# Plain weight tiles of a hybrid decoder layer: rounded by a transfer, with the low part made by a negation and an accumulating transfer, in place of a float32 tile that two engines split

## The chip, the core and the metric

The kernel runs on one core of a Trainium2 chip, in one launch. The metric is device time in microseconds, as the median of three runs. Profiles come from one profiled execution; its span runs from the first to the last instruction, and the time of that execution is a little longer.

## What is computed

One decoder layer over 16 meta tokens and 512 tokens (T = 528 columns, features on the partitions), d_model 1024, all in float32:

```python
h = h + 0.5 * swiglu(rmsnorm(h, norm_ffn1), w_ffn1_in, w_ffn1_out)      # d_ff 2816
u = rmsnorm(h, norm_mix)
fq, fk, fv, ff, rq, rk, rv, rg, ga, gb = split(u @ w_in)
y_a = forgetting_attention(qknorm(fq), qknorm(fk), fv, cumsum(log_sigmoid(ff + b)))   # 16 heads of 64
y_b = silu(rg) * head_groupnorm(retention(rotary(rq), rotary(rk), rv))                # 4 heads
h = h + (sigmoid(ga) * (y_a @ w_o_fox) + sigmoid(gb) * (y_b @ w_o_ret)) @ w_out
h = h + 0.5 * swiglu(rmsnorm(h, norm_ffn2), w_ffn2_in, w_ffn2_out)
```

The meta tokens stand ahead of the sequence; the output is that of the 512 tokens.

## The kernel before

**Products.** Each float32 operand is held as two float32r tiles: the high part (`wh`, `xh`), which is the value rounded, and the low part (`wl`, `xl`), the rest. A product is three matmuls, high by high, high by low and low by high (`mm3`, line 269, and `mm3s`, line 285). A weight piece of 1024 columns holds eight k-steps of 128; over 528 columns, in two ranges of 272 and 256, it makes 48 matmuls, over 512 columns 24.

**Weights.** All weights are cut beforehand into a list of `loads` (up to 2048 columns, kind "w" for plain or "S" for those of a Strassen-like scheme in the two SwiGLU blocks) and a list of `pieces` in the order in which TensorE takes them (lines 125 to 162). Two plain pieces make up a load of 2048 columns. `load` (line 168) brings a load as float32 into a raw tile, with SP's queue, into one of two buffers of 8 KB per partition for plain loads (tag `w`) or of two for Strassen loads (tag `wS`). `ready` (line 195) prepares the pieces up to a number: for a plain piece `split` (line 104) rounds the raw piece into `wh` on ScalarE (line 105) and subtracts on VectorE into `wl` (line 106); Strassen pieces are split in halves of 512 columns, from the raw tile or from sums that VectorE makes (`wsums`, line 184). `wh` and `wl` have four buffers each. `weights` (line 219) is called once for each piece that TensorE takes, and readies pieces up to two ahead of it.

**Order.** TensorE's order is written out by hand (`SEQ` at line 36 for the SwiGLU blocks; generators woven by costs, `weave` at line 112, for attention and retention). The other engines' orders come from a planner that takes what is ready by order of tracing, and each engine and each issuing queue runs its list in order. At the very start ScalarE's and VectorE's orders too are as traced (line 478). In the token list a and b are plain pieces of the input weights, e and l stand for two Strassen pieces each (24 matmuls per piece), and p is a piece of the output weights (640 or 768 columns).

**Names.** `fpa`, `fpb`, `fq`, `fpo` are products of the first SwiGLU block, `spa`, `sq`, `spo` those of the second; `pff`, `pq`, `pk`, `pv`, `pg`, `prq` to `prg` are projections; `q0pm`, `k0pm` the means of the q and k norms; `pzt`, `pzd` transposes in the forget gate's chain (`forget`, line 533), `z`; `S`, `P`, `PT`, `PV` attention's scores, softmax, transposes and outputs, with `ph`, `pl` the split of P transposed; `oa`, `ob`, `ow` the products with w_o_fox, w_o_ret and w_out.

**GpSimd's queue** makes constants at the start, the bias tiles of attention (`bias`, line 760: a load `B` from `negc` and an addition `Bd`), the loads of stored gates (`gate`, line 1033: `gs` from `gsp`) and of the stored residual (line 1092: `hh` from `hsp`).

**The start.** The first load, w0, comes in four quarters of 512 columns that alternate with the tiles of h on SP's queue (lines 234 to 238); n0 takes pieces 0 and 1 side by side, n1 takes pieces 2 and 3.

Of the kernel before, what the change touches and what calls it, by code (L numbers as in the profile page):

```python
# [17 lines left out]
F32 = mybir.dt.float32  # L18
F32R = mybir.dt.float32r
AF = mybir.ActivationFunctionType  # L20
ALU = mybir.AluOpType
# [4 lines left out]
S = 512  # L26
# [38 lines left out]
def layer(tc, order, hT, wf1i, wf1o, wf2i, wf2o, wmix, wsq, vecs, cs, rmask, rvec, cmask, outT):  # L65
    nc = tc.nc
    PSUM = bass.MemoryType.PSUM
    PE = mybir.EngineType.PE
    with ExitStack() as es:
        cp = es.enter_context(tc.tile_pool(name="const", bufs=1))  # L70
        wp = es.enter_context(tc.tile_pool(name="w", bufs=1))
        ap = es.enter_context(tc.tile_pool(name="a", bufs=1))
        tp = es.enter_context(tc.tile_pool(name="t", bufs=1))
        sp = es.enter_context(tc.tile_pool(name="sm", bufs=1))
# [10 lines left out]
        def atile(name, dt=F32):  # L85
            return ap.tile([128, T], dt, name=name, tag="a", bufs=NA)
# [4 lines left out]
        def f32(x):  # L91
            return x.bitcast(F32)
# [11 lines left out]
        def split(xh, xl, src):  # L104
            nc.scalar.activation(xh, src, AF.Copy)  # L105
            nc.vector.tensor_tensor(xl, src, f32(xh), ALU.subtract)  # L106
# [18 lines left out]
        loads = []  # L125
        pieces = []
# [8 lines left out]
        def feed_ffn(seq, w_in, w_out):  # L135
            at_, nxt = {}, [0] * len(PJ)
            for tok in seq:
                c, j = tok[0], int(tok[1:])
                if c == "u":
                    continue  # L140
                if c == "p":
                    n = PJ[j] * 128
                    m = nxt[j]
                    nxt[j] += 1
                    if m % 2 == 0:
                        loads.append((w_out[j * 4 + m // 2], 2 * n, "w"))
                        at_[tok] = len(loads) - 1
                    pieces.append((at_[tok], m % 2 * n, n))
                    continue
                if c in "nae":  # L150
                    loads.append((w_in[j], 2048, "S" if c == "e" else "w"))
                    at_[j] = len(loads) - 1
                cuts = {"n": [0, 1024], "a": [0], "b": [1024],
                        "e": [("A0", "S1"), ("A2", "S0")], "l": [("A1", "S2"), ("A3",)]}[c]
                pieces.extend((at_[j], x, 1024) for x in cuts)
# [4 lines left out]
        for i in range(3 * KC // 2):  # L160
            feed(wsq[i], [1024, 1024])
        feed_ffn(SEQ, wf2i, wf2o)
        raw, sums, got = {}, {}, {}
        u = [], []
        st = {"sp": None}
        at = {"l": 0, "p": 0, "u": 0}

        def load(n):
            while at["l"] < min(n, len(loads)):
                i = at["l"]  # L170
                src, w, kind = loads[i]
                if kind == "S":
                    if st["sp"] is None:
                        return
                    raw[i] = st["sp"].tile([128, 2048], F32, name=f"w{i}", tag="wS", bufs=2)
                else:
                    raw[i] = wp.tile([128, 2048], F32, name=f"w{i}", tag="w", bufs=2)
                ld = nc.sync.dma_start(raw[i][:, :w], src[:, :w])
                if i == 5:
                    with tc.issue_after(ld.ins):  # L180
                        nc.sync.dma_start(RV, rvec)
                at["l"] += 1

        def wsums(i):

            a11, a12, a21, a22 = (raw[i][:, 512 * x:512 * x + 512] for x in range(4))
            sums[i] = st["sp"].tile([128, 1536], F32, name=f"ws{i}", tag="ws", bufs=1)
            s1, s2, s4 = (sums[i][:, 512 * x:512 * x + 512] for x in range(3))
            with tc.issue_after(st["sq"].ins):
                nc.vector.tensor_tensor(s1, a21, a22, ALU.add)  # L190
            nc.vector.tensor_tensor(s2, s1, a11, ALU.subtract)
            nc.vector.tensor_tensor(a21, a11, a21, ALU.subtract)
            nc.vector.tensor_tensor(s4, a12, s2, ALU.subtract)

        def ready(n):
            while at["p"] < min(n, len(pieces)):
                i = at["p"]
                li, c, w = pieces[i]
                load(li + 2 if i >= 2 else 1)
                if li not in raw:  # L200
                    return
                if loads[li][2] == "S" and li not in sums:
                    wsums(li)
                wh = wp.tile([128, 1024], F32R, name=f"wh{i}", tag="wh", bufs=4)
                wl = wp.tile([128, 1024], F32R, name=f"wl{i}", tag="wl", bufs=4)
                got[i] = wh, wl
                at["p"] += 1
                if i < 2:
                    for x in (0, 512):
                        split(wh[:, x:x + 512], wl[:, x:x + 512], raw[li][:, c + x:c + x + 512])  # L210
                        gained(2 * i + x // 512, gn1, u, 0, "n1")
                elif loads[li][2] == "S":
                    for x, src in enumerate(c):
                        src = (raw, sums)[src[0] == "S"][li][:, 512 * int(src[1]):512 * int(src[1]) + 512]
                        split(wh[:, 512 * x:512 * x + 512], wl[:, 512 * x:512 * x + 512], src)
                else:
                    split(wh[:, :w], wl[:, :w], raw[li][:, c:c + w])

        def weights():
            i = at["u"]  # L220
            at["u"] += 1
            ready(i + 3)
            assert i in got
            return got.pop(i)

# [2 lines left out]
        nc.scalar.dma_start(VEC, vecs)  # L228
        table(LNEXP)
        h = [atile(f"h{k}") for k in range(KC)]  # L230
        w0 = wp.tile([128, 2048], F32, name="w0", tag="w", bufs=2)
        raw[0] = w0
        at["l"] = 1
        for k in range(KC):
            if k < 4:
                nc.sync.dma_start(w0[:, 512 * k:512 * k + 512], wf1i[0][:, 512 * k:512 * k + 512])
            nc.sync.dma_start(h[k], hT[:, k, :])
        load(2)
        gn1, gnm, gn2 = VEC[:, 0:8], VEC[:, 8:16], VEC[:, 16:24]
        bga = VEC[:, 24:40]  # L240
        rgn = VEC[:, 40:48]
        bfo = VEC[:, 48:49]
        qg0, kg0 = VEC[:, 49:50], VEC[:, 50:51]
        RV = cp.tile([128, 16], F32, name="RV")
        zeta, xi, xi2 = RV[:, 0:4], RV[:, 4:8], RV[:, 8:12]
        zmeta = RV[:, 12:16]
        ident = cp.tile([128, 128], F32, name="ident")
# [41 lines left out]
        def gained(k, g, u, a, name):  # L289

            x = atile(f"{name}uh{k}", F32R)
            y = atile(f"{name}ul{k}", F32R)
            nc.scalar.activation(x[:, a:T], h[k][:, a:T], AF.Copy, scale=g[:, k:k + 1])
            nc.vector.scalar_tensor_tensor(y[:, a:T], h[k][:, a:T], g[:, k:k + 1], f32(x[:, a:T]),
                                           ALU.mult, ALU.subtract)
            u[0].append(x)
            u[1].append(y)
# [203 lines left out]
        u = nu  # L501
# [10 lines left out]
        with tc.tile_pool(name="psM", bufs=1, space=PSUM, reuse_waits="tile") as pM:  # L512
# [576 lines left out]
            u = [], []  # L1089
            for m in range(KC):  # L1090
                x = atile(f"hh{m}")
# [130 lines left out]
```

## Time and profile before

| | |
|---|---|
| median of three runs | 1366.76 us (1365.56 to 1366.83) |
| profiled execution, its own time | 1366.95 us |
| its span | 1365.1 us |
| granted TensorE clock, mean | 1.000 |
| busy: TensorE / VectorE / ScalarE / GpSimd | 1347.7 / 1009.3 / 663.8 / 60.6 us |
| DMA moved | 139.41 MB, 127.31 MB of it on SP's queue |
| HBM read | 129.56 MB |

Engines in the rows: PE is TensorE's matmuls, PEld its weight loads (they overlap), DVE VectorE, ACT ScalarE, POOL GpSimd, SP SyncE; SPq and POOLq are their queues. L106 is line 106. A row of a group shows out<-in, the count, the busy time, the mean of one and the idle time of the engine ahead of them with what ended it. A row of a stretch shows for each engine how long it was busy and how many instructions (x) it ran, then the granted clock, the DMA engines' share and the rate. Matmuls are pipelined, so their own durations overlap; the distance from start to start is what a stretch's length over its count gives.

### The profile page before, as it was taken

The numbers are of one execution on the slowest core, as the hardware profiler recorded it, in microseconds if no ns is written. First come the engines' busy times: TensorE is split into PE (matmuls) and PEld (weight loads), VectorE is DVE, ScalarE is ACT, GpSimd is POOL, SyncE is SP. The second block draws the span as 40 slices with busy tenths as digits, with TensorE's granted clock in tenths as the row PEclk, the third lists the DMA queues.
The fourth block names the chain that finished last, engine by engine and source line by source line (L and its number), as shares of the span: only waits on it lengthen the run. The fifth ranks groups of instructions, "written<-read, shape, count | busy, mean of one in ns | idle before, by whom it ended". The sixth has DMA issues, their size and how long they took to land.

```text
span 1365.1 us, 22221 instructions
## 1 busy us (share of the span) xinstructions
PE 1347.7 (99%) x8871; PEld 1227.8 (90%) x8871; DVE 1009.3 (74%) x1948; ACT 663.8 (49%) x1131; POOL 60.6 (4%) x96
## 2 busy tenths in 40 slices
PE   8999999999999999999999999999999999999998
PEld 7999999999988788888888999888888989989897
DVE  7987777877778877787865777645558878888773
ACT  7433433333567677777754344544435333334331
POOL 0000000000013210110000000001100000000000
PEclk9999999999999999999999999999999999999999
DMA  7122223220623322232221212244421222232202
GB/s 281 48 92 98 82 102 139 86 105 20 211 73 116 117 78 78 94 124 94 94 78 62 94 62 100 86 155 162 162 93 63 101 104 82 101 126 99 105 27 94
DMA packets 27814, 139.41 MB, mean 102 GB/s; under 512 B 3632, under 2 KB 4016, under 8 KB 16576
## 3 DMA queue, kind: packets, MB, share of 16 engines
q1 hardware_dynamic: 24336, 127.31, 26.1%
q0 software_dynamic: 3232, 10.65, 2.6%
q8 instruction: 70, 1.15, 0.3%
q14 instruction: 32, 0.26, 0.1%
q10 hardware_dynamic: 144, 0.04, 0.0%
HBM read 129.56 MB, written 8.42 MB: 101 GB/s over the span
## 4 chain that ended last, share of the span: by engine, by line
PE 95%; DVE 3%; ACT 1%; DMA 0%; issue 0%; SPq 0%; DVEq 0%; ACTq 0%
PE fq L287 10%; PE sq L287 10%; PE fpo L277 9%; PE spo L277 9%; PE pg L277 6%; PE fpb L277 4%; PE prv L277 3%; PE fpa L277 3%; PE prg L277 3%; PE spa L277 3%; PE spb L277 3%; PE ow L277 3%; PE ob L277 3%; PE oa L277 3%; PE pv L277 3%; PE pq L277 3%
## 5 line engine op out<-in xcount | busy, mean ns | idle before, releaser
L105 ACT ACTIVATE wh<-w 128x512 fp32r<-128x512 f32 (+3 forms) x299 | 249.5, 834 | 463.5 <-PE fpo L277 69.1
L106 DVE TENSOR_TENSOR wl<-w,wh 128x512 fp32r<-128x512 f32 (+3 forms) x299 | 282.9, 946 | 68.9 <-ACT wh L105 66.6
L277 PE MATMUL fpo<-fgl,wh 128*128 128x272 f32 x352 | 71.4, 284 | 0.0
L277 PE MATMUL fpo<-fgh,wh 128*128 128x272 f32 x352 | 71.3, 284 | 0.0
L277 PE MATMUL fpo<-fgh,wl 128*128 128x272 f32 x352 | 71.3, 284 | 0.0
L277 PE MATMUL spo<-sgh,wl 128*128 128x512 f32 (+1 forms) x181 | 70.2, 388 | 0.0
L277 PE MATMUL spo<-sgh,wh 128*128 128x512 f32 (+1 forms) x181 | 70.1, 387 | 0.0
L277 PE MATMUL spo<-sgl,wh 128*128 128x512 f32 (+1 forms) x181 | 69.9, 386 | 0.0
L106 DVE TENSOR_TENSOR wl<-ws,wh 128x512 fp32r<-128x512 f32 x84 | 57.4, 683 | 0.0
L1117 DVE SCALAR_TENSOR_TENSOR hh<-spo,hh 128x512 f32<-128x512 f32 (+1 forms) x33 | 22.2, 674 | 45.5 <-PE spo L277 45.5
L106 DVE TENSOR_TENSOR pl<-PT,ph 128x512 fp32r<-128x512 f32 (+4 forms) x80 | 34.0, 432 | 28.1 <-ACT ph L105 27.5
L277 PEld LDWEIGHTS fpo<-fgh,wl 128*128 128x128 f32 x352 | 54.0, 188 | 0.0
L277 PEld LDWEIGHTS fpo<-fgh,wh 128*128 128x128 f32 x352 | 53.9, 188 | 0.0
L277 PEld LDWEIGHTS fpo<-fgl,wh 128*128 128x128 f32 x352 | 53.9, 188 | 0.0
L277 PE MATMUL pg<-n2uh,wh 128*128 128x512 f32 x128 | 53.8, 420 | 0.0
L105 ACT ACTIVATE wh<-ws 128x512 fp32r<-128x512 f32 x84 | 51.7, 616 | 0.0
L492 DVE SCALAR_TENSOR_TENSOR h<-fpo,h 128x528 f32<-128x528 f32 x32 | 22.6, 706 | 38.0 <-PE fpo L277 38.0
L277 PE MATMUL pg<-n2uh,wl 128*128 128x512 f32 x128 | 50.5, 395 | 0.0
L277 PE MATMUL pg<-n2ul,wh 128*128 128x512 f32 x128 | 50.4, 393 | 0.0
L794 ACT ACTIVATE P<-P,st 128x144 f32<-128x144 f32 (+1 forms) x64 | 36.5, 571 | 26.4 <-DVE st L790 25.5
L287 PE MATMUL fq<-n1uh,wh 128*128 128x264 f32 x168 | 47.8, 284 | 0.0
L287 PE MATMUL fq<-n1ul,wh 128*128 128x264 f32 x168 | 47.7, 284 | 0.0
(934 smaller groups left out, 4288.4 us busy)
## 6 DMA issues: line engine op xcount, KB each, us to landing
w<-in_wmix SPq DMA_DIRECT2D x32, 1024.0 KB, 4.9
w<-in_wf2i SPq DMA_DIRECT2D x22, 1024.0 KB, 4.9
w<-in_wf1i SPq DMA_DIRECT2D x21, 1024.0 KB, 4.8
w<-in_wsq SPq DMA_DIRECT2D x12, 1024.0 KB, 4.9
w<-in_wf1o SPq DMA_DIRECT2D x8, 768.0 KB, 4.2
w<-in_wf2o SPq DMA_DIRECT2D x8, 768.0 KB, 4.1
w<-in_wf1o SPq DMA_DIRECT2D x8, 640.0 KB, 4.0
w<-in_wf2o SPq DMA_DIRECT2D x8, 640.0 KB, 3.9
```

Source lines behind the costliest of these rows:

```text
L105: nc.scalar.activation(xh, src, AF.Copy)
L106: nc.vector.tensor_tensor(xl, src, f32(xh), ALU.subtract)
L277: nc.tensor.matmul(out, p[:, o:o + 128], q[:, a:b], start=first and k == 0 and i == 0, stop=last and k == nk - 1 and i == 2)
L287: nc.tensor.matmul(out, p, q, start=start and i == 0, stop=stop and i == 2)
L492: nc.vector.scalar_tensor_tensor(h[m][:, x:y], ps, 0.5, h[m][:, x:y], ALU.mult, ALU.add)
L794: last["exp"] = nc.scalar.activation(P[i][:, :w], P[i][:, :w], AF.Exp, scale=-1.0, bias=st[:, 2:3], accum_out=sm[:, 0:1])
L1117: nc.vector.scalar_tensor_tensor(h[m][:, x:y], ps, 0.5, h[m][:, x:y], ALU.mult, ALU.add)
```

## The change

Plain pieces no longer pass through a float32 tile. `begin` (new) allots a piece's `wh` and, from piece 2 on, lets GpSimd's queue load it straight from HBM into the float32r tile, by a transfer that rounds, up to six pieces ahead of TensorE. `ready`, now up to four pieces, has ScalarE write the negated `wh` into `wl`, and then GpSimd's queue issues a second transfer that adds the float32 weights from HBM to `wl`. Raw tiles remain for Strassen loads alone. `wh` has seven buffers in place of four, `wl` five in place of four, and the two raw buffers of plain loads are gone (the same 48 KB per partition in all). Pieces 0 and 1 are split as before, from two float32 tiles of the tag `wl`. The small load of RV moves from behind load 5 to the end of the first loads.

```diff
@@ -160,26 +160,24 @@
         for i in range(3 * KC // 2):
             feed(wsq[i], [1024, 1024])
         feed_ffn(SEQ, wf2i, wf2o)
-        raw, sums, got = {}, {}, {}
+        raw, sums, high, got = {}, {}, {}, {}
         u = [], []
         st = {"sp": None}
-        at = {"l": 0, "p": 0, "u": 0}
+        at = {"l": 0, "c": 0, "p": 0, "u": 0}
 
         def load(n):
             while at["l"] < min(n, len(loads)):
                 i = at["l"]
                 src, w, kind = loads[i]
-                if kind == "S":
-                    if st["sp"] is None:
-                        return
-                    raw[i] = st["sp"].tile([128, 2048], F32, name=f"w{i}", tag="wS", bufs=2)
-                else:
-                    raw[i] = wp.tile([128, 2048], F32, name=f"w{i}", tag="w", bufs=2)
-                ld = nc.sync.dma_start(raw[i][:, :w], src[:, :w])
-                if i == 5:
-                    with tc.issue_after(ld.ins):
-                        nc.sync.dma_start(RV, rvec)
                 at["l"] += 1
+                if kind == "w":
+                    raw[i] = src
+                    continue
+                if st["sp"] is None:
+                    at["l"] -= 1
+                    return
+                raw[i] = st["sp"].tile([128, 2048], F32, name=f"w{i}", tag="wS", bufs=2)
+                nc.sync.dma_start(raw[i], src)
 
         def wsums(i):
 
@@ -192,7 +190,18 @@
             nc.vector.tensor_tensor(a21, a11, a21, ALU.subtract)
             nc.vector.tensor_tensor(s4, a12, s2, ALU.subtract)
 
+        def begin(n):
+
+            while at["c"] < min(n, len(pieces)):
+                i = at["c"]
+                li, c, w = pieces[i]
+                high[i] = wp.tile([128, 1024], F32R, name=f"wh{i}", tag="wh", bufs=7)
+                at["c"] += 1
+                if i >= 2 and loads[li][2] == "w":
+                    nc.gpsimd.dma_start(high[i][:, :w], loads[li][0][:, c:c + w])
+
         def ready(n):
+            begin(n)
             while at["p"] < min(n, len(pieces)):
                 i = at["p"]
                 li, c, w = pieces[i]
@@ -201,25 +210,28 @@
                     return
                 if loads[li][2] == "S" and li not in sums:
                     wsums(li)
-                wh = wp.tile([128, 1024], F32R, name=f"wh{i}", tag="wh", bufs=4)
-                wl = wp.tile([128, 1024], F32R, name=f"wl{i}", tag="wl", bufs=4)
+                wh = high.pop(i)
+                wl = wp.tile([128, 1024], F32R, name=f"wl{i}", tag="wl", bufs=5)
                 got[i] = wh, wl
                 at["p"] += 1
                 if i < 2:
                     for x in (0, 512):
-                        split(wh[:, x:x + 512], wl[:, x:x + 512], raw[li][:, c + x:c + x + 512])
+                        split(wh[:, x:x + 512], wl[:, x:x + 512], raw[li][i][:, x:x + 512])
                         gained(2 * i + x // 512, gn1, u, 0, "n1")
                 elif loads[li][2] == "S":
                     for x, src in enumerate(c):
                         src = (raw, sums)[src[0] == "S"][li][:, 512 * int(src[1]):512 * int(src[1]) + 512]
                         split(wh[:, 512 * x:512 * x + 512], wl[:, 512 * x:512 * x + 512], src)
                 else:
-                    split(wh[:, :w], wl[:, :w], raw[li][:, c:c + w])
+
+                    nc.scalar.activation(wl[:, :w], f32(wh[:, :w]), AF.Copy, scale=-1.0)
+                    nc.gpsimd.dma_start(wl[:, :w], raw[li][:, c:c + w], accum_op=ALU.add)
 
         def weights():
             i = at["u"]
             at["u"] += 1
-            ready(i + 3)
+            begin(i + 6)
+            ready(i + 4)
             assert i in got
             return got.pop(i)
 
@@ -228,12 +240,12 @@
         nc.scalar.dma_start(VEC, vecs)
         table(LNEXP)
         h = [atile(f"h{k}") for k in range(KC)]
-        w0 = wp.tile([128, 2048], F32, name="w0", tag="w", bufs=2)
+        w0 = [wp.tile([128, 1024], F32, name=f"w0{x}", tag="wl", bufs=5) for x in "ab"]
         raw[0] = w0
         at["l"] = 1
         for k in range(KC):
             if k < 4:
-                nc.sync.dma_start(w0[:, 512 * k:512 * k + 512], wf1i[0][:, 512 * k:512 * k + 512])
+                nc.sync.dma_start(w0[k // 2][:, 512 * (k % 2):512 * (k % 2) + 512], wf1i[0][:, 512 * k:512 * k + 512])
             nc.sync.dma_start(h[k], hT[:, k, :])
         load(2)
         gn1, gnm, gn2 = VEC[:, 0:8], VEC[:, 8:16], VEC[:, 16:24]
@@ -242,6 +254,7 @@
         bfo = VEC[:, 48:49]
         qg0, kg0 = VEC[:, 49:50], VEC[:, 50:51]
         RV = cp.tile([128, 16], F32, name="RV")
+        nc.sync.dma_start(RV, rvec)
         zeta, xi, xi2 = RV[:, 0:4], RV[:, 4:8], RV[:, 8:12]
         zmeta = RV[:, 12:16]
         ident = cp.tile([128, 128], F32, name="ident")
```

## Rows read from the trace of the kernel before

**Rows 1.** The page: busy time of each engine, share of the span, instructions.

```profile
PE 1347.7 (99%) x8871; PEld 1227.8 (90%) x8871; DVE 1009.3 (74%) x1948; ACT 663.8 (49%) x1131; POOL 60.6 (4%) x96
```

**Rows 2.** Stretches: us, busy time of each engine (x), clock, DMA share, GB/s.

```profile
40.00:410.00 370.00, 367.39 (x2973) 364.23 (x2972) 287.98 (x503) 151.97 (x236) 5.90 (x11) 1.00 0.28 98
410.00:460.00 50.00, 46.75 (x320) 41.94 (x319) 43.09 (x94) 40.25 (x78) 14.96 (x17) 1.00 0.33 109
...
930.00:990.00 60.00, 60.00 (x261) 48.72 (x260) 35.94 (x47) 27.08 (x36) 9.04 (x17) 1.00 0.48 166
...
60.00:100.00 40.00, 40.00 (x331) 40.00 (x330) 34.47 (x64) 16.07 (x26) 0.00 (x0) 1.00 0.21 73
...
345.00:374.00 29.00, 29.00 (x241) 29.00 (x240) 21.19 (x29) 16.01 (x23) 0.00 (x0) 1.00 0.57 198
```

**Rows 3.** Waits of TensorE over the span: us in total, times, longest us.

```profile
PE fpa L277 <- ACT n1uh L293: 6.1, 1, 6.1
PE q2pm L635 <- ACT q2sh L105: 1.7, 1, 1.7
PE PV L850 <- DVE pl L106: 1.3, 2, 0.9
PE pzt L542 <- DVE z L538: 1.2, 1, 1.2
...
PE k0pm L636 <- DVE k0sl L106: 0.5, 1, 0.5
...
PE fpb L277 <- ACT wh L105: 0.4, 1, 0.4
...
PE PV L847 <- DVE pl L106: 0.2, 1, 0.2
```

**Rows 4.** Chain of waits, 370 to 480 us: start us, us, what.

```profile
390.23 1.22 DVE wl L106
...
397.93 1.14 DVE wl L106
...
433.92 1.65 DVE wl L106
...
453.97 0.52 DVE wl L106
...
473.42 1.23 DVE wl L106
```

**Rows 5.** Groups by form: splits of plain pieces on VectorE (line 106).

```profile
L106 DVE TENSOR_TENSOR wl<-w,wh 128x1024 fp32r<-128x1024 f32 x119 | 146.8, 1233 | 39.9 <-ACT wh L105 38.5
...
L106 DVE TENSOR_TENSOR wl<-w,wh 128x768 fp32r<-128x768 f32 x32 | 30.6, 956 | 0.0
L106 DVE TENSOR_TENSOR wl<-w,wh 128x640 fp32r<-128x640 f32 x32 | 26.1, 817 | 8.2 <-ACT wh L105 8.2
```

**Rows 6.** Timeline of the start: start us, us, engine, line, operation.

```profile
5.70 0.41 POOL L256 CAST bones<-bo 128x128 fp32r<-128x128 f32 x1
...
8.57 0.81 PE L277 MATMUL fpb<-n1uh,wh 128*128 128x272 f32 x2 [0.37 <-ACT wh L105]
...
15.42 1.06 ACT L105 ACTIVATE wh<-w 128x1024 fp32r<-128x1024 f32 x1
...
21.61 0.31 PEld L277 LDWEIGHTS fpa<-n1uh,wl 128*128 128x128 f32 x2
```

**Rows 7.** GpSimd: tile B's issues (ns min/median/max, first to last us); timeline.

```profile
L763 POOL DMA_DIRECT2D B<-negc x16: 553/553/572, 420.3 to 661.3; - x16
...
928.71 0.54 POOL L1035 DMA_DIRECT2D gs<-gsp  x1 [52.94 <-DVE gs L1081]
...
955.51 0.54 POOL L1035 DMA_DIRECT2D gs<-gsp  x1 [4.08 <-DVE ml L106]
```

**Rows 8.** DMA issues with xcount, KB each, us to landing.

```profile
w<-in_wmix SPq DMA_DIRECT2D x32, 1024.0 KB, 4.9
...
w<-in_wmix SPq DMA_DIRECT2D x1, 512.0 KB, 3.6
```

## The prediction

> **What bounds the kernel now.** I read the page's busy table first: TensorE is busy for 1347.7 of 1365.1 us, VectorE for 1009.3, ScalarE for 663.8 and GpSimd for 60.6 [rows 1]. So at most 17.4 us of the span can come from anything but faster matmuls. Then the table of stretches [rows 2] asks whether the matmul stream feels its neighbours. Matmuls of 256 to 272 columns start every 120.8 ns (40.00 us over 331) where VectorE is busy for 86% of the time and every 120.3 ns (29.00 over 241) where it is busy for 73% and the DMA share is 0.57 instead of 0.21. Those of 512 columns take 229.9 ns (60.00 over 261). The granted clock is 1.00 in all of them. A count is good to one matmul, 1% here, so I book no gain and no loss in the stream, and keep 1 us either way for it.
>
> What is left are TensorE's waits, in the list of who waited for whom [rows 3]: 6.1 us for the first operands, and 7.7 us in twelve further entries. Of these 6.0 lie behind VectorE or ScalarE between 390 and 476 us, by their tiles (z, the q and k of attention, ph and pl). The chain of waits in that stretch [rows 4] shows why: VectorE works there without a pause, and five splits of weight tiles (wl, line 106) lie on the chain, 5.76 us together. Elsewhere the weights come early enough: only 0.4 us of TensorE's waits name a weight tile (fpb on wh, at the start).
>
> **The change against 1366.95 us.** The sum stands against the profiled execution (span 1365.1, 1.85 us around it), which is 0.19 us over the median of the three runs, 1366.76. A difference under 0.2%, 2.7 us, can't be told from no change.
>
> Removed: the 183 VectorE subtractions of plain pieces (119 of 1024 columns, 32 of 768, 32 of 640), 146.8 + 30.6 + 26.1 = 203.5 us of VectorE [rows 5]. The ScalarE roundings are replaced one for one by negations of the same shape, which I price at the same 1.06 us for 1024 columns [rows 6]: nothing gained there. Wherever TensorE does not wait, VectorE's 203 us are worth nothing, for the matmul stream hides them.
>
> Term 1, the stretch of 390 to 476 us. Each split on the chain, with the wait behind it: 1.22 us stands ahead of R, z and the transpose pzt (a wait of 1.2); 1.14 ahead of k0sl (0.5); 1.65 ahead of the P operations and q2sh (1.7); 0.52 and 1.23 ahead of pl (1.3 for both) [rows 3, 4]. The smaller of each pair is 1.2 + 0.5 + 1.65 + 1.3 = 4.65. ScalarE stands next on the chain with its copies of q and k and isn't relieved, so I take three quarters, **-3.5 us**; the ends are 0, if ScalarE sets every one of these waits anyway, and -6.0, all waits of the stretch.
>
> Term 2, the start. The low part of piece 2 was ready 1.23 us after its rounding and is first used at 21.61 [rows 5, 6]. Now the negation ends at 16.48, GpSimd issues in 0.55 [rows 7], and the transfer lands: no accumulating transfer is in the trace, so its price lies between a plain 512 KB load, 3.6 us, and a 1024 KB one, 4.9 (it reads as many bytes again at its destination) [rows 8]. That gives 20.6 to 21.9: between nothing and 0.3 us late. Besides, five casting loads (pieces 2 to 6, 2.6 MB) find free buffers and leave as soon as GpSimd gets to them, in place of one 1 MB load that SP issued behind all h loads. They share the DMA engines with the last quarters of w0, for which fpb waits until 8.57, and with h. GpSimd's own order has bones at 5.70 ahead of them [rows 6]. If they come after it they delay little. If they run one for one with SP's loads from 3 us on, what arrived between 3 and 8 us takes twice as long, and fpb starts up to 5 us later. I take **+1.0 us**, nearer to the first by that row, with ends of -0.3 (VectorE's share of the start is shorter) and +5.
>
> Term 3, the supply itself: **0**, hidden by the leads. A piece of 24 matmuls lasts 24 x 123.6 ns (367.39 over 2973) = 3.0 us at 264 columns and 5.5 us at 512 [rows 2]; full pieces over 528 columns have 48 matmuls and last 5.9. The accumulating transfer of a piece may start when a buffer comes free, four pieces before its use, 11.9 us in the worst case of four Strassen pieces. It takes a negation 1.06, an issue 0.55 and a landing of 4.9, so 6.5. The casting load has two pieces, 5.9 us, ahead of its negation and takes 0.55 + 3.6 = 4.2. In throughput: from 512 to 1024 KB the landing grows by 1.3 us [rows 8], so 512 KB cost the engines 1.3 us as a cast and, by bounds, 1.3 (like a plain load) to 5.2 us (four times one) as an accumulation; I take twice, 2.6, since it has two reads for a write. Together 3.9 of 5.5 us. If the cover goes, each piece costs the excess over 5.5.
>
> The Trainium skill (Collectives: The Full Stack, section The bandwidth ceiling) says that a DMA's add is slow for its two source reads and not for the arithmetic. By it the accumulation is at twice a plain load and the sum is unchanged, while at the upper bound it would be the third rival's. No run here shows it yet.
>
> Edits at no cost: GpSimd gets 366 issues of about 0.55 us, 201 us on an engine that is busy for 4% [rows 1, 7]. Its queue is in order, so behind a cast that waits for a buffer stand the bias loads B and their additions Bd (sixteen issues from 420.3 to 661.3 us, so a head has some 16 us, more than any piece [rows 7]), the gate loads gs and the loads of hh; behind a gate load that waits stand casts. From 930 us on the gate loads wait up to 4.1 us each, well under four pieces of 5.5. The one at 928.71 waited 52.9 us for a tile that the merge's first product frees [rows 7]; the casts for that product have to stand ahead of it, or the wait would never end, so the planner puts them there. ScalarE's SiLU and softmax steps stand behind a negation that waits for its cast; that wait is 0 as long as the cast's two pieces of lead hold. SP loses loads and keeps those of the Strassen tiles, one piece earlier, and no wait of TensorE names one of them [rows 3]. The load of RV (8 KB) only moves up. The two plain pieces of w0 keep their splits.
>
> Sum: 1366.95 - 3.5 + 1.0 + 0 = 1364.45, less the 0.19 to the median: **1364.3 us**.
>
> **Rivals.** (1) The same stretch is ScalarE's: the negations cost what the roundings did and, four pieces ahead, sit ahead of more of its work. For it: 40.25 of 50 us of ScalarE are busy from 410 to 460, and the longest wait there, 1.7 us, is named as ScalarE's q2sh. Against: VectorE has 43.09 of the 50 [rows 2, 3]. Term 1 is 0: 1367.8.
> (2) All of the waits go and the start costs nothing: 1366.76 - 6.0 - 0.3 = 1360.5.
> (3) Slower: the accumulation costs four plain loads. It decides once cast and accumulation exceed 5.5 us per piece, so above 4.2 us, 3.2 times a plain load. Then a piece takes 1.3 + 5.2 = 6.5 us, and in the merge and output stage, about 880 to 990 us, sixteen such pieces are 16 us behind, and the 24 transfers of 256 KB of gs and hh (0.65 us each by the same slope) another 15.6 us; the lead of four pieces less the 10 us of latency covers some 12. That is +20, TensorE waiting on DMA there: 1384. For it: the DMA share is already 0.48 from 930 to 990 with 166 GB/s [rows 2]. Against: the slope of the landings, 512 KB in 1.3 us or some 400 GB/s [rows 8], leaves room at twice the price.
> (4) GpSimd's issuing is held by VectorE. In the trace the sixteen issues of B last 553 to 572 ns each, the first of them in the 50 us in which VectorE is busy for 43.09 [rows 2, 7]; nothing is held there. Held for one more VectorE operation, 1.2 us each, the supply still fits (7.7 of 11.9 us), but piece 2 comes that much later: 1365.5.
> The Trainium skill (SBUF — State Buffer, section SBUF: two separate sides) has this as a rule: GpSimd can't write descriptors while VectorE runs in a two-port mode. The trace doesn't show it in any of the sixteen issues of B; by the rule the sum would be rival 4's.
>
> **Chances.** Forecast 0.46 (its own range 1361.5 to 1367: faster 0.24, same 0.20, slower 0.02). Rival 1: 0.17 (same 0.10, slower 0.07, as the orders of the engines are planned anew). Rival 2: 0.11, faster. Rival 3: 0.19, slower, half of it beyond 1381. Rival 4: 0.07, same. Faster 0.35, same 0.37, slower 0.28. The range is 1360.5 to 1381, which leaves out the worse half of rival 3 and the rim of rival 2. Nothing is faster by more than the 17.4 us in which TensorE isn't busy.
>
> **What the profile will show.** Right: VectorE about 200 us less busy, ScalarE as before, GpSimd with 366 issues, HBM reads up by 85 MB, TensorE's busy time within 1 us of 1347.7, and the waits of pzt, k0pm and PV from 390 to 476 us halved while fpa or fpb at the start wait a little longer. Wrong: TensorE waiting for a DMA into wl or wh outside the start (term 3, rival 3), accumulations landing in over 7 us, q2pm and PV waiting as long as before with ScalarE full (term 1), or a start in which the first matmul of piece 2 comes after 24 us (term 2).

## The result, and the profile after

The changed kernel takes **1377.15 us** (median of 4 runs, 1375.54 to 1380.66) beside 1366.8 for the kernel before: a ratio of 1.0081, interval 1.006 to 1.0101. It is 10.4 us slower, where 1364.3 and a gain were forecast. The profiled execution took 1377.54 us, with a span of 1375.8.

The page's busy line and the row of GpSimd's DMA queue (packets, MB, share of 16 engines' span):

```profile
PE 1350.0 (98%) x8871; PEld 1229.2 (89%) x8871; DVE 815.5 (59%) x1765; ACT 658.1 (48%) x1131; POOL 319.4 (23%) x462
...
q0 software_dynamic: 55936, 181.59, 60.3%
```

Against [rows 1] VectorE lost 193.8 us and GpSimd gained 258.8; ScalarE kept its load, as forecast. TensorE is 2.3 us busier with the same 8871 matmuls, where the forecast allowed 1. HBM reads rose by 85.5 MB to 215.02. Now the stretches, with the columns of [rows 2]; the first line is the kernel before, the other two are the changed kernel:

```profile
0.00:40.00 40.00, 33.48 (x248) 32.77 (x249) 30.25 (x44) 27.72 (x41) 2.12 (x14) 1.00 0.65 240
...
0.00:40.00 40.00, 26.81 (x176) 25.89 (x177) 16.10 (x23) 23.38 (x35) 11.91 (x28) 0.91 1.01 305
880.00:1000.00 120.00, 120.00 (x551) 97.98 (x551) 42.19 (x78) 53.78 (x78) 40.14 (x62) 1.00 0.92 232
```

The start has a DMA share of 1.01 in place of 0.65 and a granted clock of 0.91, with only 176 matmuls in 40 us in place of 248. From 880 to 1000 us, where the third rival expected the collapse, the DMA share is 0.92 and TensorE is still busy throughout. The waits of TensorE, as in [rows 3]:

```profile
PE fpa L290 <- DMA wl<-in_wf1i: 6.9, 1, 6.9
PE fpa L290 <- ACT n1uh L306: 6.1, 1, 6.1
PE pvt L692 <- DVE vr L688: 3.2, 5, 0.8
PE k2pm L648 <- ACT k2sh L105: 2.1, 1, 2.1
PE pff L290 <- issue: 1.6, 1, 1.6
PE k0pm L649 <- DVE k0sl L106: 1.0, 1, 1.0
```

Two entries are new and large: 6.9 us for a low part at the start, and five waits of `pvt` for `vr`. The 1.2 us of `pzt` and the 1.7 of `q2pm` in [rows 3] are gone, `k2pm` has come in their place.

To see where the time went I lined the matmuls of the two traces up, since TensorE's order is the same in both. The table gives the start of the same matmul less its start in the kernel before, in us, at five places (their times in the kernel before), for this kernel and for the experiments that follow:

```
place (us)          40    386    476    700   1364
after             +8.7   +9.4   +7.5  +11.7  +10.8
e1_hold           +7.8   +8.0   +8.1  +12.2  +11.2
e6_noadd          +7.4   +7.3   +4.6   +8.7   +7.8
e3_vr             +8.4   +8.4  +11.4  +11.4  +10.6
e2_start          -0.4   -0.4   -2.8   +1.0    0.0
e5_nosub          -0.8   -0.8   -3.8   +0.3   -0.1
e7_start_vr3       0.0   +2.6   +1.9   +2.0   +1.0
e9_before_vr3     -0.2   -0.2   -1.2   -0.4   -0.4
e14_neg3          +1.7   +7.1   +4.8   +4.9   +3.9
e13_neg           -0.2   -0.3   -2.4   -2.3   -3.3
```

The first line splits the loss of the profiled execution: +8.7 by 40 us, +0.7 up to 386, -1.9 in the stretch of Term 1, +4.2 from 476 to 700, -0.9 after that. The start in rows (timelines of GpSimd, ScalarE, GpSimd, TensorE, and last the shortest, median and longest landing of the five casts):

```profile
5.92 2.90 POOL L201 DMA_DIRECT2D wh<-in_wf1i  x5
...
12.65 0.74 ACT L306 ACTIVATE n1uh<-h,VEC 128x528 fp32r<-128x528 f32 x1 [1.53 <-DMA h<-in_hT]
14.59 0.74 ACT L306 ACTIVATE n1uh<-h,VEC 128x528 fp32r<-128x528 f32 x1 [1.20 <-DMA h<-in_hT]
16.64 0.74 ACT L306 ACTIVATE n1uh<-h,VEC 128x528 fp32r<-128x528 f32 x1 [1.32 <-DMA h<-in_hT]
...
18.89 1.05 ACT L227 ACTIVATE wl<-wh 128x1024 fp32r<-128x1024 f32 x1
...
20.24 0.90 POOL L228 DMA_DIRECT2D wl<-in_wf1i  x1 [11.43 <-DVE acc L316]
...
28.57 0.81 PE L290 MATMUL fpa<-n1uh,wl 128*128 128x272 f32 x2 [6.90 <-DMA wl<-in_wf1i]
29.18 0.64 PE L290 MATMUL fpa<-n1uh,wh 128*128 128x272 f32 x2
...
32.60 0.41 PE L290 MATMUL fpa<-n1uh,wl 128*128 128x272 f32 x2
...
DMA to landing us min/median/max: 7.7/9.9/16.4
```

The five casts leave at 5.92, right behind `bones` as [rows 6] let expect. But the negation of piece 2 runs only at 18.89, where the rounding it replaces ran at 15.42 [rows 6]; ahead of it in ScalarE's order the last three `n1uh` waited 4.05 us together for their tiles of h, against 0.15 in the kernel before. Its cast was not what it lacked: in the trace the first of the five casts is the one that lands after 7.7 us, at 13.6. The accumulating transfer is issued at 20.24, and TensorE, which wanted the tile at 21.67, gets it 6.9 us later. The matmul pairs from 28.57 to 32.26 last about 0.64 us each instead of 0.41: the granted clock is 0.51 from 25.6 to 32.5 us, the 1.2 GHz level, and this half clock takes another 1.8 us.

### The profile page after: what moved, and what is told of

The parts are those of the page before. It is cut to its first block, busy times and chain, and to the rows that moved or that the text cites. A ratio compares the mean times of both kernels' runs of the same rounds, so it can differ in the third digit from the quotient of the medians.

```text
span 1375.8 us, 22630 instructions
## 1 busy us (share of the span) xinstructions
PE 1350.0 (98%) x8871; PEld 1229.2 (89%) x8871; DVE 815.5 (59%) x1765; ACT 658.1 (48%) x1131; POOL 319.4 (23%) x462
## 3 DMA queue, kind: packets, MB, share of 16 engines
q0 software_dynamic: 55936, 181.59, 60.3%
HBM read 215.02 MB, written 8.42 MB: 162 GB/s over the span
## 4 chain that ended last, share of the span: by engine, by line
PE 89%; ACT 4%; issue 3%; DVE 2%; DMA 1%; POOL 1%; POOLq 0%; ACTq 0%
PE fq L300 10%; PE sq L300 10%; PE fpo L290 9%; PE spo L290 9%; PE pg L290 5%; PE prv L290 3%; PE oa L290 3%; PE prg L290 3%; PE spa L290 3%; PE spb L290 3%; PE ow L290 3%; PE ob L290 3%; PE fpa L290 3%; PE fpb L290 3%; PE pq L290 3%
## 5 line engine op out<-in xcount | busy, mean ns | idle before, releaser
L227 ACT ACTIVATE wl<-wh 128x1024 fp32r<-128x1024 f32 (+2 forms) x183 | 175.5, 960 | 160.5 <-PE prg L290 23.2
L105 ACT ACTIVATE wh<-w 128x512 fp32r<-128x512 f32 x112 | 70.6, 630 | 255.9 <-PE fq L300 60.9
L106 DVE TENSOR_TENSOR wl<-w,wh 128x512 fp32r<-128x512 f32 x112 | 76.5, 683 | 14.9 <-issue 14.6
L228 POOL DMA_DIRECT2D wl<-in_wmix x65 | 57.3, 881 | 108.2 <-ACT wl L227 94.5
L201 POOL DMA_DIRECT2D wh<-in_wmix x65 | 36.4, 560 | 183.6 <-PE pv L290 32.5
```

The source lines that it names most:

```text
L201: nc.gpsimd.dma_start(high[i][:, :w], loads[li][0][:, c:c + w])
L227: nc.scalar.activation(wl[:, :w], f32(wh[:, :w]), AF.Copy, scale=-1.0)
L228: nc.gpsimd.dma_start(wl[:, :w], raw[li][:, c:c + w], accum_op=ALU.add)
```

## The experiments

**Theories.** Mine: the start costs 8.7 us because the chain of cast, negation and accumulation is longer than the lead of piece 2, and the rest is VectorE's new order, which puts `vr` late; the supply outside the start is covered. Rivals: the five casts only have to leave later; the accumulation as such is too dear; the waits of `pvt` come from the transfers.

**e1_hold.** The casts of the start stand behind the landing of the last tile of h.

```diff
+ if i == 2:
+     st["hold"] = nc.gpsimd.tensor_copy(hold, h[KC - 1][:, 0:1])
+ with tc.issue_after(st["hold"].ins):
      nc.gpsimd.dma_start(high[i][:, :w], loads[li][0][:, c:c + w])
```

> The kernel after, with its first five casting loads held on GpSimd until the last tile of h has landed. Theory A (the casts take the DMA engines from the tiles of h, ScalarE in its traced order comes to the negation of piece 2 at 18.9 instead of 15.4 us, and the low part is late by that): the negation is back at about 15.4 us, TensorE's wait of 6.9 us for wl shrinks by 3.5 us or more, to 3.4 or less, and the time falls from 1377.2 to about 1372 to 1373. Rival B (the adding transfer alone is late, some 8 us from issue to landing behind whatever else is queued, whenever it is issued): held casts then compete with it instead, the wait stays at 5 to 7 us and the time stays within 2 us of 1377.2.

1378.69 us (4 runs), ratio 1.009, 1.0073 to 1.0106: no gain, the outcome of Rival B. Timelines of GpSimd and ScalarE:

```profile
12.67 2.90 POOL L205 DMA_DIRECT2D wh<-in_wf1i  x5
20.20 0.90 POOL L232 DMA_DIRECT2D wl<-in_wf1i  x1 [4.62 <-ACT wl L231]
...
18.83 1.06 ACT L231 ACTIVATE wl<-wh 128x1024 fp32r<-128x1024 f32 x1 [3.98 <-DMA wh<-in_wf1i]
```

The tiles of h come in time now, but the cast, issued at 12.67, lands at 18.83 and the negation starts as late as in the changed kernel; TensorE waits 6.1 us for the low part. From the cast's issue to the low part it takes some 15 us: 6.2 for the cast among its four neighbours, 1.06 for the negation, an issue and some 7 for the accumulation. The first use is 9 us after that cast's issue. So holding all five casts back repairs nothing. Other orders were not tried: in the changed kernel the cast of piece 2 was in by 13.6 us, and neither its negation ahead of the late `n1uh` nor the casts of pieces 2 and 3 alone ahead of h had a run. By 40 us this kernel stands 0.9 us better than the changed one; a stretch of half clock from 455 to 458.5 us (last section) takes more than that away.

**e2_start.** Pieces 2 and 3 come as float32 through SP's queue and are split as before; the casts begin with piece 4, behind the landing of these loads.

```diff
+ raw[1] = [wp.tile([128, 1024], F32, name=f"w1{x}", tag="wl", bufs=5) for x in "ab"]
+ for x in range(2):
+     nc.sync.dma_start(raw[1][x], wf1i[1][:, 1024 * x:1024 * x + 1024])
...
+ elif i < 4:
+     split(wh, wl, raw[li][i - 2])
```

> The kernel after, with pieces 2 and 3 brought and split as in the kernel before (float32 by SP behind h, rounding and subtraction) and the casts from piece 4 on held until that load has landed; all later pieces as in the kernel after. Theory (8.6 of the 10.8 us that the last matmul comes later were lost at piece 2, 6.9 as the wait and 1.7 as matmuls at half the clock behind it): no wait for a DMA into wl at the start, the granted clock of the first 40 us back from 0.91 to 1.00, and the time at 1368 to 1369.5. Rival (the supply by transfers costs time everywhere, and the start only shows it first): the wait moves on to piece 4 or 5, or spreads, and the time stays above 1373.

1367.39 us (10 runs), ratio 1.0007, 0.9996 to 1.0017, a little under what the theory gave: the loss is gone, and nothing is won. The largest entry of TensorE's waits after that for the first operands, and the first 40 us:

```profile
PE pvt L701 <- DVE vr L697: 2.8, 5, 0.6
```

```profile
0.00:40.00 40.00, 33.60 (x251) 32.88 (x252) 26.84 (x43) 30.20 (x45) 10.20 (x26) 1.00 0.98 296
```

The wait for a DMA and the half clock of the start have vanished although 181 of the 183 accumulations are still there, all but those of pieces 2 and 3, and the DMA share of the start is 0.98. So the loss at the start is the latency of the chain ahead of piece 2; a DMA share near 1 costs TensorE nothing there once that chain has more time. In the table 2.8 us are won by 476, and 3.8 lost again by 700: `pvt` waits for `vr`.

**e5_nosub.** The kernel before without VectorE's subtractions for plain pieces: the tile of the high part serves as the low part too (the output lacks the low parts of the plain weights). No transfer is changed.

```diff
- split(wh[:, :w], wl[:, :w], raw[li][:, c:c + w])
+ nc.scalar.activation(wh[:, :w], raw[li][:, c:c + w], AF.Copy)
```

> The kernel before, with the subtraction of the plain pieces from piece 2 on left out and the high part used in place of the low one (the output lacks the low part of those weights); loads, roundings and matmuls are unchanged, and no transfer is added. It shows what VectorE's relief is worth by itself. Theory (VectorE's order is planned anew without the subtractions): the waits of pzt and PV shrink by 2 to 4 us, five waits of pvt for vr come back with 4 us together, and the time is 1365.5 to 1369 against 1366.8. Rival (the late vr comes with GpSimd's queue and the transfers): no waits of pvt for vr, and the time is 1362.5 to 1364.5.

1367.72 us (10 runs), ratio 1.0007, 0.9998 to 1.0016. One wait of TensorE:

```profile
PE pvt L680 <- DVE vr L676: 3.2, 5, 0.9
```

VectorE is busy for 824.8 us, 184.5 less than in [rows 1], and the kernel is no faster. In the table 3.0 us are won in attention's first part (2.4 in e2_start) and 4.1 given back between 476 and 700 (3.8), with no accumulation anywhere. So these waits come from VectorE's order and not from the transfers. VectorE's timeline around one `vr`, of the kernel before:

```profile
501.51 0.38 DVE L796 RECIPROCAL sm<-sm 128x1 f32<-128x1 f32 x2
501.81 0.69 DVE L675 TENSOR_TENSOR vr<-pv,R 128x528 f32<-128x528 f32 x1
502.41 0.43 DVE L790 CUSTOM_DVE_ANT_0 P<-S,B 128x272 f32<-128x272 f32 x1
```

and of the changed kernel:

```profile
509.12 0.16 DVE L809 RECIPROCAL sm<-sm 128x1 f32<-128x1 f32 x1 [0.26 <-ACT P L807]
509.20 0.69 DVE L652 TENSOR_TENSOR k3v<-k3pm,epsR 128x528 f32<-128x528 f32 x1
509.81 0.15 DVE L809 RECIPROCAL sm<-sm 128x1 f32<-128x1 f32 x1
509.88 0.42 DVE L803 CUSTOM_DVE_ANT_0 P<-S,B 128x272 f32<-128x272 f32 x1
...
510.23 0.70 DVE L688 TENSOR_TENSOR vr<-pv,R 128x528 f32<-128x528 f32 x1
```

Before, `vr` follows the two reciprocals at once and the P step of 272 columns comes after it. In the changed kernel `k3v` and that P step stand ahead of it. That fits a planner that takes what is ready by order of tracing (with VectorE free earlier other work is ready earlier), but its decisions are not in the trace. TensorE's fixed order wants the transposes of `vr` up to 0.8 us sooner, five times.

**e3_vr.** The changed kernel with `vr` moved up in VectorE's order, for all pairs of heads.

```diff
+ with tc.high_priority(offset=HP):
      nc.vector.tensor_tensor(vr, v, R, ALU.mult)
```

> The kernel after, with the VectorE product vr of each head pair given the priority that the softmax steps have, and nothing else. Theory (with the subtractions gone the planner put vr behind the first softmax step of the next row block; TensorE waits for it at pvt in five head pairs, 3.2 us by the waits and 4.4 us by the shift of the matmuls): these waits go and the time falls by 3 to 4.5 us, to 1373 to 1374. Rival (vr is late since ScalarE or the transfers hold VectorE's inputs): vr moves but another wait takes its place, 1376 to 1378.

1377.74 us (4 runs), ratio 1.0079, 1.0064 to 1.0094. The waits of TensorE:

```profile
PE fpa L290 <- DMA wl<-in_wf1i: 5.8, 1, 5.8
PE k0pm L649 <- DVE k0sl L106: 2.6, 1, 2.6
PE k2pm L648 <- ACT k2sh L105: 2.1, 1, 2.1
PE k2pm L649 <- DVE k2sl L106: 1.8, 1, 1.8
```

`pvt` is gone, and `k0pm` and `k2pm` have grown from 1.0, 2.1 and 0.5 to 2.6, 2.1 and 1.8: in the first pairs of heads what is moved up pushes the splits of k back. The rival's outcome: by the table the matmuls lose 3.0 us between 386 and 476 where the changed kernel wins 1.9, and lose nothing from 476 to 700 where it loses 4.2. Of those 4.9 us up to 476 the longer waits are 2.9; behind them the granted clock is 0.51 from 459.7 to 463.2 us, where the changed kernel has 1.00, and the rest fits this half clock.

**e6_noadd.** The changed kernel with the second transfer as a rounding transfer without the addition (the low part then holds the rounded weights).

```diff
- nc.gpsimd.dma_start(wl[:, :w], raw[li][:, c:c + w], accum_op=ALU.add)
+ nc.gpsimd.dma_start(wl[:, :w], raw[li][:, c:c + w])
```

> The kernel after with the second transfer of each plain piece as a rounding transfer into the low tile, without the addition (the low part then holds the rounded weights). Theory (an addition costs the DMA engines two reads for one write: 4096-byte packets of it last 328 ns against 174 of a rounding one): the second transfer lands in about 5 us in place of 7.0, the queue's share falls from 60% to about 42%, TensorE's wait at piece 2 shrinks by 2 to 3 us but doesn't go, and the time is 1373 to 1375. Rival (the addition is as cheap as a copy and the landing is all waiting in the queue): landings and the wait at piece 2 as they were, 1376 to 1378.

1374.49 us in one execution. Its row of the DMA queue and one landing, against those of the changed kernel, whose landings and GpSimd issues come first:

```profile
wh<-in_wmix POOLq DMA_DIRECT2D x65, 512.0 KB, 4.8
wl<-in_wmix POOLq DMA_DIRECT2D x65, 512.0 KB, 7.0
...
gs<-gsp POOLq DMA_DIRECT2D x16, 256.0 KB, 7.1
```

```profile
L228 POOL DMA_DIRECT2D wl<-in_wmix x65 | 57.3, 881 | 108.2 <-ACT wl L227 94.5 <-issue 8.7 <-ACT vm L105 3.9
L201 POOL DMA_DIRECT2D wh<-in_wmix x65 | 36.4, 560 | 183.6 <-PE pv L290 32.5 <-PE prv L290 28.1 <-PE pg L290 27.6
```

and of e6_noadd:

```profile
q0 software_dynamic: 55936, 181.59, 43.7%
```

```profile
wl<-in_wmix POOLq DMA_DIRECT2D x65, 512.0 KB, 5.0
```

This prices the addition. GpSimd's queue took 60.3% of 1375.8 us with it and 43.7% of 1372.7 without it: 829.6 and 599.9 us, a difference of 229.7 for 183 accumulations. In e6_noadd the 366 rounding transfers took 599.9 less some 35 us for what the queue carried before (2.6% on its page), 282 us for 183. So an accumulation costs (282 + 230) / 282 = 1.8 rounding transfers, lands 2.0 us later and takes GpSimd 0.88 us to issue instead of 0.56. The wait at the start shrinks from 6.9 to 5.3 us only, less than the 2 to 3 us expected: most of it is the chain of two transfers, not the addition.

**e7_start_vr3 and e9_before_vr3.** e2_start with the priority for `vr`, only in the pairs after the first three, and as a control the kernel before with the same priority.

```diff
+ with tc.high_priority(offset=HP if p > 2 else 0):
      nc.vector.tensor_tensor(vr, v, R, ALU.mult)
```

> The kernel after with pieces 2 and 3 brought and split as before (as in the earlier run on the start) and with the softmax steps' priority for the product vr of the head pairs 3 to 7 alone, so that the first three pairs, whose k and q norms lost what the others won when all had it, keep their order. Theory (the relief of VectorE is worth some 3 to 4 us by 475 us, and the order of vr gave it back): no waits of pvt for vr, the matmuls end some 4 us earlier than in the kernel before, and the time is 1362.5 to 1364, faster than both kernels. Rival (what pvt no longer waits for is waited for elsewhere, as when all pairs had the priority): 1366.5 to 1368.

> The kernel before with the same priority of vr for the head pairs 3 to 7, as a control. Theory (in the kernel before vr comes in time, so the priority has nothing to win): within 1.5 us of 1366.8. Rival (the priority is worth 3 to 4 us by itself, whatever VectorE has to do): 1363 to 1364.

e7_start_vr3: 1364.94 us (11 runs), ratio 0.999, 0.9982 to 0.9999: no wait of `pvt` is left, but the gain is under the one expected. The control: 1368.32 (11 runs), 1.0013, 1.0004 to 1.0022, so the priority wins nothing where VectorE still has the subtractions. A second series of e7_start_vr3 beside the next run:

> The same kernel as e7_start_vr3, on the chip of e14_neg3, so that the two stand side by side and the small gain of e7_start_vr3 is measured a second time. If the gain over the kernel before is real: 1364 to 1365.5, ratio 0.998 to 0.9995. If it was chance: ratio 0.9995 to 1.0005.

1364.18 us (11 runs), ratio 0.9987, 0.9978 to 0.9995: the small gain is real. Its executions lie far apart (1363.36 to 1368.25). Of the 22 of both series, the eleven with a mean granted clock of 1.000 take 1363.06 to 1364.94 us, the eleven below that 1364.58 to 1368.25. The profiled one of the first series, its longest with 1367.6, shows where the clock is lost. ScalarE, VectorE and TensorE at the end of the first SwiGLU block:

```profile
373.74 1.06 ACT L233 ACTIVATE wl<-wh 128x1024 fp32r<-128x1024 f32 x1 [2.44 <-issue]
374.71 0.72 ACT L315 ACTIVATE n2uh<-h,VEC 128x528 fp32r<-128x528 f32 x1
...
376.76 0.70 DVE L514 SCALAR_TENSOR_TENSOR h<-fpo,h 128x528 f32<-128x528 f32 x1
...
377.57 0.78 PE L299 MATMUL pff<-n2uh,wh 128*128 128x272 f32 x2 [2.05 <-issue]
378.14 0.65 PE L299 MATMUL pff<-n2ul,wh 128*128 128x272 f32 x2
```

A negation stands ahead of `n2uh` and waited 2.44 us. The row names no releaser; in the trace its cast, issued at 364.63, lands at 373.67. Behind that wait `n2ul` and then `h`, which reads a PSUM bank out; `pff`, by the order of the rows, wants that bank and starts 2.05 us late. After this pause its pairs last 0.65 us instead of 0.41 for 3 us (granted clock 0.51 from 377.5 to 381). In e2_start, with the same order there, the wait was 0.85 us and no half clock followed. The changed kernel has the same chain, +0.7 us by 386, without half clock.

**e14_neg3 and e13_neg.** Both set the negations of that stretch behind the `n2uh` of the output tile before; e14_neg3 also asks for the last ones a piece later.

```diff
+ with tc.issue_after(st["n2"]) if st.get("n2") else ExitStack():
      nc.scalar.activation(wl[:, :w], f32(wh[:, :w]), AF.Copy, scale=-1.0)
...
- nc.scalar.activation(x[:, a:T], h[k][:, a:T], AF.Copy, scale=g[:, k:k + 1])
+ xi = nc.scalar.activation(x[:, a:T], h[k][:, a:T], AF.Copy, scale=g[:, k:k + 1])
+ st["n2"] = xi.ins if name == "n2" and k < KC - 1 and a == 0 else None
```

> Starts from e7_start_vr3. In the last output group of the first feed-forward, each negation now stands behind the n2uh activation of the output tile before it, and the last tiles ask for negations three pieces ahead instead of four. In e7_start_vr3's profile the negation that waited 2.44 us for its cast (start 373.74) had n2uh, n2ul and the read-out of the last output tile's PSUM bank queued behind it, and pff waited 2.05 us for that bank and then ran for 3 us at half clock. If a negation waiting ahead of the activation is the cause, pff's wait is gone (under 0.4 us), the half clock after it too, and the median is 1.5 to 2.5 us under e7_start_vr3: 1362.5 to 1363.5. Rival: pff waits anyway, for the last h and n2uh (as in the kernel before, where the wait there is short but the chain is the same), and the median stays at 1364.5 to 1365.5.

1366.93 us (12 runs), ratio 1.0003, 0.9993 to 1.0012: a miss. The bank's wait fell to 0.85 us, but the low part of `pff`'s weights came 2.8 us late, with half clock from 380 to 387. At this place the lead of four pieces is needed.

> As e14_neg3, but the negations keep their lead of four pieces; each only goes behind the n2uh activation of the output tile before it. In e14_neg3's profile n2uh came in time (pff's wait on the PSUM bank 0.8 us instead of 2.05), but the negations, a piece later as well, made the low part of pff's weights 2.8 us late, with half clock behind it. Here the negation of that piece stands about 3.6 us earlier than in e14_neg3 and should land before its use. If so: no wait of pff on a DMA, its bank wait 0.8 or less, and a median of 1362.5 to 1364. Rival: the negation that now stands ahead of the last n2uh waits for its cast and hands the delay on, as in e7_start_vr3: 1364 to 1366.

**1363.29 us** (7 runs, 1363.12 to 1364.13), ratio 0.9971, 0.9959 to 0.9982. ScalarE and TensorE at the same place:

```profile
372.43 0.74 ACT L316 ACTIVATE n2uh<-h,VEC 128x528 fp32r<-128x528 f32 x1 [1.42 <-DVE h L516]
...
373.61 1.99 ACT L234 ACTIVATE wl<-wh 128x1024 fp32r<-128x1024 f32 x2
377.45 1.06 ACT L234 ACTIVATE wl<-wh 128x1024 fp32r<-128x1024 f32 x1 [1.85 <-DMA wh<-in_wmix]
378.42 0.72 ACT L316 ACTIVATE n2uh<-h,VEC 128x528 fp32r<-128x528 f32 x1
...
376.14 0.48 PE L300 MATMUL pff<-n2uh,wh 128*128 128x272 f32 x2 [0.85 <-ACT wl L234]
376.46 0.41 PE L300 MATMUL pff<-n2ul,wh 128*128 128x272 f32 x2
```

`n2uh` of 372.43 is no longer behind a waiting negation, `pff` waits 0.85 us, and the pairs run at 0.41 at once. The negation that waits 1.85 us now holds up only the last `n2uh`, which is wanted late in `pff`. This version beats the kernel before by 4 us and the change by 14. Not all that it has over e7_start_vr3's profile comes from this edit: in the table 2.9 us are gone by 386, and 1.4 more by 476, where e7_start_vr3 has a second stretch of half clock, from 449.2 to 452.7, behind a wait of 1.23 us for `k2pm`. Here that wait is 1.26 us and no half clock follows; no run shows why.

## Why the prediction was wrong

**Term 2 failed, and with it the sign.** It took +1.0 with an end of +5; the start cost 8.7. The step that failed is the time of piece 2's low part, in two sizes: that the negation would end at 16.48, and the landing, "between a plain 512 KB load, 3.6 us, and a 1024 KB one, 4.9". The negation ended at 19.94, and the accumulation, issued at 20.24, served TensorE at 28.57, 8.3 us later. Against the late end of my sum, 21.9, these are 6.6 us: 3.5 by the negation and the rest by issue and landing. I priced the accumulation by landings of a kernel whose stretches show DMA shares of 0.21 to 0.57 [rows 2]; e2_start, which takes the chain away from pieces 2 and 3, takes the 8.7 us away. I left the negation where the rounding had stood. I did say that the casts share the DMA engines with h, but gave that no price of its own: the tiles of h came late, and ScalarE's order made the negation wait behind them, although its cast was in by 13.6. With h in time (e1_hold) the cast was the late one, 6.2 us beside its four neighbours. The end of +5 was made for late quarters of w0 (`fpb`), which did not come; piece 2, for which I allowed 0.3, was the loss. My sign for this, a first matmul of piece 2 after 24 us, did not show it: that matmul uses the high part and came at 21.0. And this late piece cost more than its wait: 1.8 us of half clock came on top.

**Term 1** was right about VectorE's relief in its stretch and incomplete. Of -3.5 forecast, -1.9 came in the changed kernel, -2.4 in e2_start and -3.0 in e5_nosub, within the ends. `pzt` and `q2pm` lost their waits as the chain of [rows 4] said; `k0pm`'s, which should have halved, went from 0.5 to 1.0. What I missed is that the planner makes VectorE's order anew when 183 entries leave it: from 476 to 700 `vr` comes late, +4.2, a loss that the sum held at nothing. In the stretch itself `k2pm` now waits 2.1 us for ScalarE's split of k. The sentence "wherever TensorE does not wait, VectorE's 203 us are worth nothing" holds; that they cost nothing there doesn't follow. In e5_nosub the same relief, without any new transfer, is worth nothing in the end where I had 3.5 us.

**Term 3 held for TensorE.** Outside the start it waits for no DMA in the changed kernel, with a DMA share of 0.92 from 880 to 1000 us. The landings were longer than priced: accumulations of 512 KB land after 6.7 to 7.8 us by the medians of their groups, where I took 4.9 and named over 7 as a sign of being wrong, and the lead covered it. The accumulation costs 1.8 rounding transfers where I took 2. By the queue's shares a 512 KB cast takes the engines 282 x 512 / 83456 = 1.7 us (the 183 pieces have 83,456 KB) and an accumulation 3.1, so a piece has 4.9 of 5.5 us, not 3.9: closer to the edge than I wrote. The Trainium skill (Collectives: The Full Stack, section The bandwidth ceiling), which puts a DMA's add down to its two source reads, agrees with 1.8 here. One cover was not complete: ScalarE's steps "behind a negation that waits for its cast" were priced at 0 while the cast's two pieces of lead, 5.9 us, hold, with 4.2 for the cast. At the end of the first SwiGLU block they don't: in the changed kernel a cast issued at 373.32 lands at 381.90, 8.6 us later. The wait costs +0.7 there and 2.6, with the half clock, in e7_start_vr3's profile; in e13_neg's it is gone.

**The rivals.** The slower rival's place was wrong: not throughput at 880 us but latency at 20 us. The measured time lies in the stated range because that rival stretched it, which is luck as to the cause. Rival 1 holds in part: `k2pm`'s 2.1 us are ScalarE's, yet the stretch gained 1.9. Rival 4's delay of a VectorE operation, 1.2 us per issue, did not come: 65 casts are issued in 0.56 us each and 65 accumulations in 0.88, on the mean, while VectorE is 59% busy. The Trainium skill (SBUF — State Buffer, section SBUF: two separate sides) lets VectorE's two-port mode block descriptor writing; no row here shows an issue held by it, and the longer 0.88 us go with the addition: without it GpSimd is busy for 252.5 us on e6_noadd's page, 66.9 less, 0.37 us for each of the 183.

## What to carry to other kernels

Before a load is replaced by a chain of dependent transfers, add up the chain's latency at the first place that uses it, with landings taken from the busiest stretch and with what stands ahead of each step in its engine's order, and keep the old path for as many pieces as that chain is long. Work taken off an engine that a planner fills is not free to take away: look at which of its instructions the fixed order of another engine wants next, and where a new wait on an in-order queue stands ahead of them. Here the same idea was worth -4 us once the first two transferred pieces, `vr` and the negations ahead of `n2uh` were put right, one by one, by where the same matmul stood in both traces. What the order of `n2uh` alone would bring to the kernel before was not tried.

## What the runs showed of the hardware that was not expected

A pause of TensorE of 2.05 us (e7_start_vr3) and one of 6.9 us (the changed kernel) were each followed by 3 to 3.7 us of matmul pairs at 0.64 us instead of 0.41, one of 0.85 us (e13_neg) by none. The length of the pause alone doesn't decide it. The same wait of `k2pm` for ScalarE's split, 2.12 us in e1_hold and 2.10 in the changed kernel, was followed by half clock in the first and by full clock in the second (columns of [rows 2]):

```profile
455.00:458.50 3.50, 3.08 (x11) 2.41 (x12) 3.05 (x7) 2.40 (x4) 1.90 (x3) 0.51 0.98 255
...
456.10:459.60 3.50, 2.98 (x16) 2.43 (x17) 3.44 (x8) 3.31 (x6) 1.90 (x3) 1.00 0.99 238
```

In e7_start_vr3 a wait of 1.23 us there was enough, in e13_neg one of 1.26 was not. So part of a difference of 1 to 2 us between two profiled executions here can be the clock and not the edit.

And some small transfers slow most under the new traffic: `gs`, 256 KB, lands after 7.1 us, where it took 3.1 in the kernel before, while the loads of the SwiGLU inputs, 1024 KB, go from 4.8 and 4.9 to 5.1 and 5.6. No wait of TensorE names `gs`.
